# A streaming group-mean subtraction: whole-row tiles, six in-place tiles for four, one sum buffer for two

## The chip, the cores and the metric

The kernel runs on one core of a Trainium2 chip. The metric is the device time in microseconds (us) of that core; profile spans are one to two us shorter than the timed figure of the same kernel. Each kernel was timed in rounds together with the kernel before, on the same chip. A run is marked slow when it is over 1.5% above the fastest of its kernel; the ratios use the other, fast runs alone. The granted clock reads 1.0 in every run here, the slow ones too.

## The reference

```python
x: (8, 4096, 2112) float32, stride 4
pooled    = x.reshape(8, 1024, 4, 2112).mean(axis=2)
upsampled = np.repeat(pooled, 4, axis=1)
return x - upsampled
```

Every group of four neighbouring rows loses its mean. That is 276.8 MB in, 276.8 MB out and very little arithmetic.

## The kernel before

A tile holds 128 groups, one a partition, each group's four rows (33,792 bytes, contiguous in memory) in a line: 64 tiles. SyncE issues the load, VectorE makes three adds and one subtraction in place, ScalarE's queue issues the store. The first and last tile are cut into four quarters by columns.

```python
io_pool  = ctx.enter_context(tc.tile_pool(name="io", bufs=4))
sum_pool = ctx.enter_context(tc.tile_pool(name="sum", bufs=2))
# ... work: whole tiles; the first and the last in EDGE_CHUNKS = 4 column quarters
for g0, gsz, c0, cw in work:
    x_tile = io_pool.tile([P, STRIDE, cw], mybir.dt.float32)
    nc.sync.dma_start(out=x_tile[:gsz], in_=xg[g0:g0 + gsz, :, c0:c0 + cw])
    s = sum_pool.tile([P, cw], mybir.dt.float32)
    nc.vector.tensor_add(out=s[:gsz], in0=x_tile[:gsz, 0, :], in1=x_tile[:gsz, 1, :])
    nc.vector.tensor_add(out=s[:gsz], in0=s[:gsz], in1=x_tile[:gsz, 2, :])
    nc.vector.tensor_add(out=s[:gsz], in0=s[:gsz], in1=x_tile[:gsz, 3, :])
    nc.vector.scalar_tensor_tensor(out=x_tile[:gsz], in0=..., scalar=-1.0 / STRIDE,
                                   in1=x_tile[:gsz], op0=mult, op1=add)   # cut
    nc.scalar.dma_start(out=og[g0:g0 + gsz, :, c0:c0 + cw], in_=x_tile[:gsz])
```

The framework puts in the waits and orders each engine's instructions. With two sum buffers it interleaves two tiles on VectorE.

## Time and profile before

| | before |
|---|---|
| time, median of 3 runs | 1337.71 us (1335.13 to 1340.23) |
| profile span | 1336.5 us |
| DMA over the span | 414 GB/s |
| VectorE busy | 1011.6 us, 76% |

Two views of the kernel before that the prediction doesn't show. The first is the chain that ended last, by engine. The second is the list of DMA issues; its last column is the median time in us from the issue of a transfer to its landing, when all its bytes have arrived.

```profile
DMA 73%; DVE 22%; issue 4%; SPq 0%; DVEq 0%
...
x_tile<-in_x_dram SPq DMA_DIRECT2D x62, 4224.0 KB, 23.1
out_dram<-x_tile ACTq DMA_DIRECT2D x62, 4224.0 KB, 24.1
```

Keep the last two numbers: a load takes 23.1 us and a store 24.1 us, while a tile passes every 20.6 us (990 us of the middle over 48 tiles). So (23.1 + 24.1) / 20.6 = 2.3 whole-tile transfers are outstanding on average, loads and stores together. This number carries the document.

### The profile page before, as it was taken

What the parts mean: (1) busy time and instruction counts of PE and PEld (TensorE: products, weight loads), DVE (VectorE), ACT (ScalarE), POOL (GpSimd) and SP (SyncE); (2) the same over time, 40 slices, a digit from 0 to 9 for tenths busy, and PEclk for the clock granted to TensorE, in tenths of its full rate; (3) what the DMA queues carried; (4) which work ended last, traced back from release to release, by engine and by line L of the source; (5) the groups of instructions that cost most, each with busy time, mean ns of one, the idle gap of its engine ahead of it and who ended that gap; (6) DMA issues with size and microseconds to landing.
All of it is one profiled execution on the core that took longest, in us unless ns stands there. A gap on an engine that the chain in (4) does not pass through costs nothing.

```text
span 1336.5 us, 724 instructions
## 1 busy us (share of the span) xinstructions
DVE 1011.6 (76%) x280; POOL 0.2 (0%) x4
## 2 busy tenths in 40 slices
DVE  5967886787776878695968678776878678796874
POOL 0000000000000000000000000000000000000000
DMA  9999999999999999999999999999999999999987
GB/s 361 383 436 436 430 429 405 417 427 403 436 433 406 417 431 422 433 419 435 405 411 435 420 408 432 392 421 419 408 432 410 434 436 405 436 409 407 433 357 310
DMA packets 26309, 553.70 MB, mean 414 GB/s; under 512 B 2240, under 2 KB 2240, under 8 KB 10432
## 3 DMA queue, kind: packets, MB, share of 16 engines
q1 hardware_dynamic: 13152, 276.83, 50.0%
q10 hardware_dynamic: 13152, 276.83, 48.7%
q14 instruction: 5, 0.04, 0.0%
HBM read 276.82 MB, written 276.82 MB: 414 GB/s over the span
## 4 chain that ended last, share of the span: by engine, by line
DMA 73%; DVE 22%; issue 4%; SPq 0%; DVEq 0%
DMA x_tile<-in_x_dram 40%; DMA out_dram<-x_tile 33%; DVE x_tile L56 16%; DVE s L50 3%; DVE s L53 3%; DVE s L54 1%; SPq L47 0%; DVEq L50 0%; DVEq L56 0%
## 5 line engine op out<-in xcount | busy, mean ns | idle before, releaser
L56 DVE SCALAR_TENSOR_TENSOR x_tile<-s,x_tile 128x8448 f32<-128x8448 f32 (+1 forms) x70 | 573.7, 8196 | 0.3
L50 DVE TENSOR_TENSOR s<-x_tile 128x2112 f32<-128x2112 f32 (+1 forms) x70 | 151.7, 2167 | 318.6 <-DMA x_tile<-in_x_dram 318.6
L53 DVE TENSOR_TENSOR s<-s,x_tile 128x2112 f32<-128x2112 f32 (+1 forms) x70 | 151.4, 2162 | 0.3
L54 DVE TENSOR_TENSOR s<-s,x_tile 128x2112 f32<-128x2112 f32 (+1 forms) x70 | 151.4, 2162 | 0.3
L79 POOL MEMSET const-uint8-127<- 128x1 uint8 x1 | 0.1, 103 | 0.0
L79 POOL MEMSET const-bfloat16-1.0<- 128x1 bf16 x1 | 0.1, 102 | 0.0
L79 POOL MEMSET const-float32-0.0<- 128x1 f32 x1 | 0.1, 99 | 0.2 <-issue 0.2
L79 POOL MEMSET const-float32-1.0<- 128x1 f32 x1 | 0.1, 99 | 0.0
## 6 DMA issues: line engine op xcount, KB each, us to landing
x_tile<-in_x_dram SPq DMA_DIRECT2D x62, 4224.0 KB, 23.1
out_dram<-x_tile ACTq DMA_DIRECT2D x62, 4224.0 KB, 24.1
x_tile<-in_x_dram SPq DMA_DIRECT2D x8, 1056.0 KB, 8.9
out_dram<-x_tile ACTq DMA_DIRECT2D x8, 1056.0 KB, 11.3
```

The source lines that it names most:

```text
L50: nc.vector.tensor_add(out=s[:gsz], in0=x_tile[:gsz, 0, :], in1=x_tile[:gsz, 1, :])
L53: nc.vector.tensor_add(out=s[:gsz], in0=s[:gsz], in1=x_tile[:gsz, 2, :])
L54: nc.vector.tensor_add(out=s[:gsz], in0=s[:gsz], in1=x_tile[:gsz, 3, :])
L56: nc.vector.scalar_tensor_tensor(out=x_tile[:gsz], in0=s[:gsz, None, :].to_broadcast([gsz, STRIDE, cw]), scalar=-1.0 / STRIDE, in1=x_tile[ ...
L79: nc = _bacc.Bacc("TRN2", target_bir_lowering=False, num_devices=1)
```

## The change

The intent of the change: keep more transfers in flight (six tiles), give VectorE one tile at a time so that it holds only one, and drop the small edge transfers. Six tiles and two sum buffers don't fit together: the build then wants 16.5 kB per partition where 9.84 are left. The diff, cut to its core:

```diff
-    io_pool = ctx.enter_context(tc.tile_pool(name="io", bufs=4))
-    sum_pool = ctx.enter_context(tc.tile_pool(name="sum", bufs=2))
+    io_pool = ctx.enter_context(tc.tile_pool(name="io", bufs=IO_BUFS))   # IO_BUFS = 6
+    sum_pool = ctx.enter_context(tc.tile_pool(name="sum", bufs=1))
-    EDGE_CHUNKS = 4
-    ... (work list with quartered first and last tile)
-    for g0, gsz, c0, cw in work:
-        x_tile = io_pool.tile([P, STRIDE, cw], mybir.dt.float32)
-        nc.sync.dma_start(out=x_tile[:gsz], in_=xg[g0:g0 + gsz, :, c0:c0 + cw])
+    for g0 in range(0, G, P):
+        x_tile = io_pool.tile([P, W], mybir.dt.float32)
+        nc.sync.dma_start(out=x_tile[:gsz], in_=xg[g0:g0 + gsz])
     ... (the same three adds and the same subtraction)
```

More of the change, by code (lines that the diff above doesn't have):

```diff
@@ L9 @@
 STRIDE = 4
+IO_BUFS = 6
 @with_exitstack
@@ L23 @@
     G = (B * S) // STRIDE
-    xg = x.rearrange("b (g f) d -> (b g) f d", f=STRIDE)
-    og = out.rearrange("b (g f) d -> (b g) f d", f=STRIDE)
-    n_gtiles = (G + P - 1) // P
-    io_pool = ctx.enter_context(tc.tile_pool(name="io", bufs=4))
-    sum_pool = ctx.enter_context(tc.tile_pool(name="sum", bufs=2))
-    EDGE_CHUNKS = 4
-    work: list[tuple[int, int, int, int]] = []
-    for gt in range(n_gtiles):
-        g0 = gt * P
-        gsz = min(P, G - g0)
-        if gt in (0, n_gtiles - 1):
-            cw = D // EDGE_CHUNKS
-            for ci in range(EDGE_CHUNKS):
-                work.append((g0, gsz, ci * cw, cw))
-        else:
-            work.append((g0, gsz, 0, D))
-    for g0, gsz, c0, cw in work:
-        x_tile = io_pool.tile([P, STRIDE, cw], mybir.dt.float32)
-        nc.sync.dma_start(out=x_tile[:gsz], in_=xg[g0:g0 + gsz, :, c0:c0 + cw])
-        s = sum_pool.tile([P, cw], mybir.dt.float32)
-        nc.vector.tensor_add(
-            out=s[:gsz], in0=x_tile[:gsz, 0, :], in1=x_tile[:gsz, 1, :]
-        )
-        nc.vector.tensor_add(out=s[:gsz], in0=s[:gsz], in1=x_tile[:gsz, 2, :])
-        nc.vector.tensor_add(out=s[:gsz], in0=s[:gsz], in1=x_tile[:gsz, 3, :])
+    W = STRIDE * D
+    xg = x.rearrange("b (g f) d -> (b g) (f d)", f=STRIDE)
+    og = out.rearrange("b (g f) d -> (b g) (f d)", f=STRIDE)
+    io_pool = ctx.enter_context(tc.tile_pool(name="io", bufs=IO_BUFS))
+    sum_pool = ctx.enter_context(tc.tile_pool(name="sum", bufs=1))
+    for g0 in range(0, G, P):
+        gsz = min(P, G - g0)
+        x_tile = io_pool.tile([P, W], mybir.dt.float32)
+        nc.sync.dma_start(out=x_tile[:gsz], in_=xg[g0:g0 + gsz])
+        rows = x_tile[:gsz].rearrange("p (f d) -> p f d", f=STRIDE)
+        s = sum_pool.tile([P, D], mybir.dt.float32)
+        nc.vector.tensor_add(out=s[:gsz], in0=rows[:, 0, :], in1=rows[:, 1, :])
+        for f in range(2, STRIDE):
+            nc.vector.tensor_add(out=s[:gsz], in0=s[:gsz], in1=rows[:, f, :])
         nc.vector.scalar_tensor_tensor(
-            out=x_tile[:gsz],
-            in0=s[:gsz, None, :].to_broadcast([gsz, STRIDE, cw]),
+            out=rows,
+            in0=s[:gsz, None, :].to_broadcast([gsz, STRIDE, D]),
             scalar=-1.0 / STRIDE,
-            in1=x_tile[:gsz],
+            in1=rows,
             op0=mybir.AluOpType.mult,
@@ L63 @@
         )
-        nc.scalar.dma_start(out=og[g0:g0 + gsz, :, c0:c0 + cw], in_=x_tile[:gsz])
+        nc.scalar.dma_start(out=og[g0:g0 + gsz], in_=x_tile[:gsz])
 _INS = ['x']
```

## The prediction

> **What bounds the kernel now.** I read first the busy shares and the DMA rows of the page, then the chain of waits, then the stretches of the span, then the order on VectorE.
>
> ```profile
> span 1336.5 us, 724 instructions
> DVE 1011.6 (76%) x280; POOL 0.2 (0%) x4
> ...
> DMA packets 26309, 553.70 MB, mean 414 GB/s; under 512 B 2240, under 2 KB 2240, under 8 KB 10432
> q1 hardware_dynamic: 13152, 276.83, 50.0%
> q10 hardware_dynamic: 13152, 276.83, 48.7%
> ```
>
> The two queues (q1 loads, q10 stores) are busy 98.7% of the span, VectorE 76%. But 414 GB/s is a mean, so busy is not the same as fast. The stretches show where it is lost; their last two columns are the DMA busy share and GB/s.
>
> ```profile
> 0.00:60.00 60.00, 43.98 (x24) 0.20 (x4) 1.00 0.95 369
> 60.00:240.00 180.00, 134.76 (x35) 0.00 (x0) 1.00 1.00 426
> 240.00:1230.00 990.00, 755.29 (x193) 0.00 (x0) 1.00 1.00 420
> 1230.00:1280.00 50.00, 38.42 (x12) 0.00 (x0) 1.00 1.01 422
> 1280.00:1336.50 56.50, 39.11 (x20) 0.00 (x0) 1.00 0.80 316
> 110.00:150.00 40.00, 40.00 (x12) 0.00 (x0) 1.00 1.00 433
> ```
>
> The last row is an undisturbed stretch: 433 GB/s. At that rate 553.70 MB take 1278.7 us, so 1336.5 - 1278.7 = 57.8 us are lost. By stretch, length x (1 - rate/433): 8.9 at the start, 2.9, 29.7 in the middle, 1.3, and 15.3 at the end. Whether the middle loss can be had back is the whole question, because there the share reads 1.00.
>
> The trace's packet records answer it. A 33,792-byte packet (one partition's row of a tile) takes 1.251 us for the most part; some load packets take up to 2.9 us. They come in bursts: 13 bursts cost 1.0 to 1.5 us each over all 16 engines, some 17 us together, 12 smaller ones about 9 us. Pairing issues with landings, the large bursts stand where both queues had run dry. One of them:
>
> ```profile
> 232.31 8.95 DVE L56 SCALAR_TENSOR_TENSOR x_tile<-s,x_tile 128x8448 f32<-128x8448 f32 x1
> 240.80 0.33 SPq L47 DMA_DIRECT2D x_tile<-in_x_dram  x1
> 241.18 2.35 DVE L54 TENSOR_TENSOR s<-s,x_tile 128x2112 f32<-128x2112 f32 x1
> 241.29 0.34 ACTq L64 DMA_DIRECT2D out_dram<-x_tile  x1
> 243.45 2.35 DVE L50 TENSOR_TENSOR s<-x_tile 128x2112 f32<-128x2112 f32 x1
> ```
>
> At 240.7 a store lands and the only other load in flight has its last packets out; new load and new store are issued within half a microsecond, and that 10 us stretch moves 375 GB/s instead of 433. The cause is buffers: each load waits for a store.
>
> ```profile
> SPq L47 <- DMA out_dram<-x_tile: 1285.2, 66, 25.4
> ```
>
> Counting issues and landings, for about 1010 of the 1336 us only one load is outstanding. Two of the four tiles are often held by VectorE, because with two sum buffers its instructions interleave two tiles:
>
> ```profile
> 165.56 8.95 DVE L56 SCALAR_TENSOR_TENSOR x_tile<-s,x_tile 128x8448 f32<-128x8448 f32 x1
> 174.43 2.35 DVE L53 TENSOR_TENSOR s<-s,x_tile 128x2112 f32<-128x2112 f32 x1
> ...
> 183.44 2.36 DVE L50 TENSOR_TENSOR s<-x_tile 128x2112 f32<-128x2112 f32 x1 [6.65 <-DMA x_tile<-in_x_dram]
> 185.71 2.35 DVE L54 TENSOR_TENSOR s<-s,x_tile 128x2112 f32<-128x2112 f32 x1
> 187.98 2.35 DVE L53 TENSOR_TENSOR s<-s,x_tile 128x2112 f32<-128x2112 f32 x1
> 190.25 8.95 DVE L56 SCALAR_TENSOR_TENSOR x_tile<-s,x_tile 128x8448 f32<-128x8448 f32 x1
> ```
>
> The tile in work at 174.43 needs two adds and the subtraction, 2.4 + 2.4 + 9.0, so could be out at 188.2. It waits in order behind the next tile's first add (183.44), which waits for that tile's load, and ends at 199.2: a buffer held 11 us for nothing.
>
> **What the Trainium skill says.** "DMA: Bandwidth & Descriptors", section "Queues, rings and completion order": each engine alternates between queues that have work, a packet at a time. The trace agrees: from 250 to 260 us both queues moved 2.16 MB. The same page, "Where 436 GB/s comes from", gives a ceiling of 435.2 GB/s; the undisturbed 433 lies just under it, so I treat 433 as the end of the road. "SBUF — State Buffer", "SBUF: two separate sides", holds that DMA and compute engines don't slow each other; at 110 to 150 us VectorE is busy 40.00 of 40.00 and the DMA still makes 433. "Perfetto Trace Analysis", "DMA Optimizations", says splitting transfers may let some start sooner if DMA engines are idle: the argument for the quartered edge tiles, weighed below.
>
> **The change part by part.**
> Quartered edges go. Bytes are the same. Their 8192 packets of 2,112 bytes cost 46.8 us of DMA time (86 ns typical) where whole rows take 2 x 2 x 128 x 1.251 / 16 = 40.0: 6.8 us saved. What is lost is the early first store and short tail.
> Start: four quarter loads fill all four buffers, so the load queue is dry by 14 us and refills late; 8.9 us lost. After, six whole loads are issued at once. First packets at 2.2 us as before; I allow 1.5 for a cold burst. First tile lands near 13.7; VectorE needs 16.1 a tile (the tile begun at 32.93 hands over at 49.10); first store about 30, while 60 us of loads are queued. No gap: loss 3.7 in place of 8.9.
> Middle: two queues with work share 433 GB/s, so a tile passes every 19.98 us (8.65 MB / 433) against 990 / 48 = 20.6 now. VectorE's dependent chain of 16.1 fits, so one tile at a time costs nothing there. Working the first tiles through by hand (store 1 from 32 to 52, store 2 to 72, tile finishes at 46, 62, 78, 94, 110), about two stores, three loads and one tile in VectorE are outstanding from 130 us on, so the load queue never runs dry. The 17 us of large bursts and the idle gaps (29.7 + 2.9 + 1.3 = 33.9, minus 25 in bursts = 9) go; of the 9 us of small bursts, which stand at store handovers, I keep 5.
> End: when the last load lands (T), the store of two tiles earlier has about 9 us left, the next queues behind it to T + 19, and the last tile leaves VectorE at T + 16, its packets ready by T + 18. So the store queue covers the 16 us of VectorE and no gap opens; 1.4 us from last packet to end, as now.
> Sum: 1278.7 + 3.7 + 5 + 1.4 = 1288.8 us of span; runs are timed 1.2 above it (1337.7 against 1336.5): 1290.
>
> **The rivals.**
> 1. DMA already full: 98.7% busy leaves 1.3%, about 1320. For it: the page's share. Against: the share counts slowed packets as busy; GB/s says 4.3% is open. It would hold if the slow bursts came from the memory and not from dry queues; then some 25 us return and the time is 1305 to 1315.
> 2. The edges cost more than I think. If only one store is outstanding at the end, the DMA idles 8 us while VectorE works on the last tile, plus 2 for the issue: 1300. With VectorE two tiles behind, another 16: 1316. Against: at 16.1 per 20.0 it keeps up.
> 3. VectorE becomes the bound: 64 x 16.1 = 1030 plus a first load of 14 and last store of 14, 1058; far off, so it can't set the end.
>
> **Range and chances.** A floor is 1278.7 + 2.2 + 1.4 + 1.2 = 1283.5; little can come out below. Up, residual bursts (up to 25) and tail (10) are not likely both. 1283 to 1308 holds 8 in 10. Faster by over 2% means under 1311: 0.91; within 2%: 0.085; slower: 0.005, as nothing on the bound resource is added.
>
> **What would show it.** Right: the middle at 430 GB/s or more with few packets above 1.3 us; whole-tile loads landing 50 us or more after issue rather than 23 (queued, harmless); VectorE's order one tile at a time with its wait still on loads; some 18,400 packets (64 x 2 x (128 + 16 short ones)) instead of 26,309; start and end each losing under 6 us. Wrong: a middle still near 420 (rival 1), or a last 50 us well below 400 GB/s with the DMA idle during the last subtraction (rival 2).

## The result, and the profile after

The changed kernel takes 1286.62 us, median of 4 runs (1286.50 to 1286.83). The kernel before, over the runs beside it, takes 1336.42 (1327.48 to 1340.23). The ratio is 0.9639, 95% interval 0.9604 to 0.9674. A ratio here is the mean time of one kernel's fast runs over that of the other's of the same rounds, so not quite the ratio of the medians. The new kernel is also steadier: its runs spread over 0.3 us, those of before over almost 13.

Totals and DMA of the changed kernel:

```profile
span 1284.7 us, 674 instructions
DVE 1026.1 (80%) x256; POOL 0.2 (0%) x4
...
DMA packets 18437, 553.70 MB, mean 431 GB/s; under 512 B 2048, under 2 KB 2048, under 8 KB 2048
```

VectorE is busy 14.5 us longer than before and the kernel is 52 us shorter by the spans. The same bytes went at 431 GB/s rather than 414. By stretch (last two columns: DMA busy share and GB/s):

```profile
0.00:60.00 60.00, 46.56 (x12) 0.20 (x4) 1.00 0.98 415
...
240.00:1230.00 990.00, 795.66 (x198) 0.00 (x0) 1.00 1.00 433
1230.00:1280.00 50.00, 32.40 (x9) 0.00 (x0) 1.00 1.00 431
```

The middle row read "1.00 1.00 420" before and reads "1.00 1.00 433" now: the busy share didn't move at all, the rate did. A share of 1.00 is not a full DMA.

The issues and the chain of the changed kernel:

```profile
x_tile<-in_x_dram SPq DMA_DIRECT2D x64, 4224.0 KB, 59.6
out_dram<-x_tile ACTq DMA_DIRECT2D x64, 4224.0 KB, 43.8
```

```profile
DVE 80%; another core or an unknown queue 17%; DMA 1%; issue 1%; DVEq 0%
```

A load now takes 59.6 us, two and a half times as long, and the kernel is faster: the loads wait in line, and the line is what keeps the DMA full. Outstanding are (59.6 + 43.8) / 20.0 = 5.2 transfers. The chain of waits moved from "DMA 73%" to "DVE 80%". Its "unknown queue" is the loads: the list of waits of the changed kernel has VectorE idle for 237.3 us, 18% of the span, all of it for x_tile<-in_x_dram. Whether VectorE has become the bound is asked of an experiment below.

VectorE now does one tile at a time: first add, two adds, subtraction, then the next tile.

```profile
29.23 2.36 DVE L43 TENSOR_TENSOR s<-x_tile 128x2112 f32<-128x2112 f32 x1
31.62 4.75 DVE L45 TENSOR_TENSOR s<-s,x_tile 128x2112 f32<-128x2112 f32 x2
36.40 8.96 DVE L46 SCALAR_TENSOR_TENSOR x_tile<-s,x_tile 128x8448 f32<-128x8448 f32 x1
45.40 2.36 DVE L43 TENSOR_TENSOR s<-x_tile 128x2112 f32<-128x2112 f32 x1
```

### The profile page after: what moved, and what is told of

Its sections match the earlier page's. It is cut to its first block, busy times and chain, and to the rows that moved or that the text cites. A ratio compares the mean times of both kernels' runs of the same rounds, so it can differ in the third digit from the quotient of the medians.

```text
span 1284.7 us, 674 instructions
## 1 busy us (share of the span) xinstructions
DVE 1026.1 (80%) x256; POOL 0.2 (0%) x4
## 2 busy tenths in 40 slices
DMA packets 18437, 553.70 MB, mean 431 GB/s; under 512 B 2048, under 2 KB 2048, under 8 KB 2048
## 4 chain that ended last, share of the span: by engine, by line
DVE 80%; another core or an unknown queue 17%; DMA 1%; issue 1%; DVEq 0%
DVE x_tile L46 45%; DVE s L45 24%; DVE s L43 12%; DMA x_tile<-in_x_dram 1%; DVEq L43 0%
## 5 line engine op out<-in xcount | busy, mean ns | idle before, releaser
L46 DVE SCALAR_TENSOR_TENSOR x_tile<-s,x_tile 128x8448 f32<-128x8448 f32 x64 | 573.3, 8958 | 2.2
L43 DVE TENSOR_TENSOR s<-x_tile 128x2112 f32<-128x2112 f32 x64 | 150.9, 2358 | 237.5 <-DMA x_tile<-in_x_dram 237.3
L45 DVE TENSOR_TENSOR s<-s,x_tile 128x2112 f32<-128x2112 f32 x128 | 301.8, 2358 | 4.4
## 6 DMA issues: line engine op xcount, KB each, us to landing
x_tile<-in_x_dram SPq DMA_DIRECT2D x64, 4224.0 KB, 59.6
out_dram<-x_tile ACTq DMA_DIRECT2D x64, 4224.0 KB, 43.8
```

The lines of the kernel that those rows point to most:

```text
L43: nc.vector.tensor_add(out=s[:gsz], in0=rows[:, 0, :], in1=rows[:, 1, :])
L45: nc.vector.tensor_add(out=s[:gsz], in0=s[:gsz], in1=rows[:, f, :])
L46: nc.vector.scalar_tensor_tensor(out=rows, in0=s[:gsz, None, :].to_broadcast([gsz, STRIDE, D]), scalar=-1.0 / STRIDE, in1=rows, op0=mybir. ...
```

## The experiments

My theory: a tile's buffer goes through load, hold by VectorE (from the landing of the load to the issue of the store), and store. With n buffers and a tile every 20 us, (20 n - hold) / 20 transfers are outstanding. If there are few, both queues run dry from time to time, and the DMA loses time in the dry spell and in the slow packets after it. (The experiments show the first part, that few outstanding transfers cost time; the part on dry spells and slow packets is argued, see the end of the next section.) Measured in the traces, the mean hold between a fifth and nine tenths of the tiles is 34.3 us before and 16.6 us after. The rivals: the number of tiles alone counts; the interleaved order alone counts; the small edge packets are to blame; the slow bursts come from the memory, whatever the queues do; VectorE sets the end.

**One sum buffer, nothing else.**

```diff
-    sum_pool = ctx.enter_context(tc.tile_pool(name="sum", bufs=2))
+    sum_pool = ctx.enter_context(tc.tile_pool(name="sum", bufs=1))
```

> The kernel before with one sum buffer instead of two, nothing else (four tiles, quartered edges). My theory: a tile slot's round is load + hold by VectorE + store, and the DMA runs dry when too few transfers are outstanding; before, four slots x 20.6 us = 82.5 us of round, of which VectorE holds 34.3 us, so 2.33 transfers are outstanding. With one tile at a time the hold falls to about 17 us, so (80 - 17)/20 = 3.15 outstanding: the middle (240 to 1230 us) at 428 GB/s or more, time 1295 to 1305 (the quartered start still loses 9 us). Rival 'only the number of tiles counts': 1330 to 1340, as before. Rival 'VectorE loses by taking tiles one at a time': over 1340.

Measured: 1300.99 us, ratio 0.9764 (0.9713 to 0.9815). The hold fell to 16.3 us. The middle, and the whole-tile issues:

```profile
240.00:1230.00 990.00, 791.80 (x199) 0.00 (x0) 1.00 1.00 433
```

```profile
x_tile<-in_x_dram SPq DMA_DIRECT2D x62, 4224.0 KB, 31.8
out_dram<-x_tile ACTq DMA_DIRECT2D x62, 4224.0 KB, 31.7
```

(31.8 + 31.7) / 20.0 = 3.2 outstanding, and the middle is full with four tiles. So the number of tiles alone doesn't decide.

**Five tiles, nothing else.**

```diff
-    io_pool = ctx.enter_context(tc.tile_pool(name="io", bufs=4))
+    io_pool = ctx.enter_context(tc.tile_pool(name="io", bufs=5))
```

> The kernel before with five tiles instead of four (two sum buffers kept; six do not fit beside them). My theory: a fifth slot pays for the second tile that VectorE holds: (5 x 20 - 34.3)/20 = 3.3 outstanding transfers, so the same as one sum buffer with four tiles: 1293 to 1305, within 5 us of that run, while VectorE still interleaves two tiles. Rival 'the interleaving itself delays the stores and sets the pace': 1325 or more.

Measured: 1296.32 us, ratio 0.9714 (0.9676 to 0.9753).

```profile
240.00:1230.00 990.00, 780.33 (x199) 0.00 (x0) 1.00 1.00 433
```

```profile
x_tile<-in_x_dram SPq DMA_DIRECT2D x62, 4224.0 KB, 28.8
out_dram<-x_tile ACTq DMA_DIRECT2D x62, 4224.0 KB, 35.7
```

VectorE still interleaves two tiles and holds each 33.5 us, as before, but (28.8 + 35.7) / 20.0 = 3.2 are outstanding, and the middle is just as full. So the interleaving doesn't hurt by itself; it costs one buffer. A fifth tile pays that, and one sum buffer saves it. The two parts of the change are two ways to the same 433 GB/s.

**Whole rows at the edges, nothing else.**

```diff
-    EDGE_CHUNKS = 4
+    EDGE_CHUNKS = 1
```

> The kernel before with its edge tiles whole instead of quartered, nothing else. My theory: the middle stays at 420 GB/s with its slow bursts; start and DMA time of the small packets gain some 5 to 10 us, the end may lose as much because one store at most is queued: 1325 to 1342. Rival 'the small packets or the mixed tile sizes set off the dry spells': under 1310.

Measured: 1326.53 us, ratio 0.9942 (0.9917 to 0.9966).

```profile
0.00:60.00 60.00, 46.63 (x12) 0.20 (x4) 1.00 0.99 413
...
240.00:1230.00 990.00, 756.32 (x193) 0.00 (x0) 1.00 1.00 422
```

The start gains 60 x (413 - 369) / 433 = 6.1 us; the middle stays as slow as before (hold 34.4 us, 2.3 outstanding). The small packets didn't cause the dry spells.

**Three tiles, with whole rows and one sum buffer.**

```diff
-IO_BUFS = 6
+IO_BUFS = 3
```

> The changed kernel with three tiles instead of six. My theory: (3 x 20 - 17)/20 = 2.15 outstanding transfers, about as few as before (2.33), so the slow bursts and gaps come back: middle 410 to 422 GB/s, time 1320 to 1345, although VectorE takes one tile at a time and all tiles are whole. Rival 'the single sum buffer and whole rows are what took the loss away, tiles beyond what VectorE needs are idle': under 1300.

Measured: ratio 0.9993 (0.9966 to 1.0020), 20 runs from 1322.47 to 1347.53, the four from 1343.04 up marked slow. The profiled run was one of these, so I ran it again.

> The three-tile run again for a profile in the fast state (before: fast runs at 0.9993 of the kernel before, profile slow at 1342.5). Expected: span 1322 to 1340, middle 415 to 421 GB/s, packet bursts as in the kernel before. Rival 'the bursts of that profile belong to the slow state': middle 430 or more.

Measured: ratio 1.0005 (0.9972 to 1.0038); this profile is a fast run, span 1328.5.

```profile
240.00:1230.00 990.00, 778.23 (x193) 0.00 (x0) 1.00 1.00 423
```

```profile
x_tile<-in_x_dram SPq DMA_DIRECT2D x64, 4224.0 KB, 23.0
out_dram<-x_tile ACTq DMA_DIRECT2D x64, 4224.0 KB, 22.6
```

This is the kernel before in another dress: three tiles with a hold of 16.3 us have as few transfers outstanding, (23.0 + 22.6) / 20.4 = 2.2, as four tiles with a hold of 34.3, and the same time. The middle (423) came out 2 GB/s above what I had written. The time beyond 1.251 us (the usual time of a packet) of all packets, divided by the 16 engines, is 30.9 us in this trace, as in the kernel before. Neither whole rows nor one sum buffer keeps the loss away.

**Four tiles, with whole rows and one sum buffer** (the same line set to 4).

> The changed kernel with four tiles instead of six. My theory: (4 x 20 - 16.3)/20 = 3.2 outstanding transfers, as in the run with one sum buffer only, so the middle is at 433 GB/s; whole rows at the edges take back most of the 10 us by which that run (1301.0) is behind the changed kernel: 1287 to 1294. Rival 'the tiles five and six are needed': 1300 or more.

Measured: 1290.38 us (1290.15 to 1290.46), ratio 0.9662 (0.9641 to 0.9683); middle 433 GB/s. Tiles five and six are worth under 4 us, at the end: with four, the rate of 1230 to 1280 us is 398 GB/s against 431 with six.

**Quartered edges, with six tiles and one sum buffer.**

```diff
-    io_pool = ctx.enter_context(tc.tile_pool(name="io", bufs=4))
-    sum_pool = ctx.enter_context(tc.tile_pool(name="sum", bufs=2))
+    io_pool = ctx.enter_context(tc.tile_pool(name="io", bufs=6))
+    sum_pool = ctx.enter_context(tc.tile_pool(name="sum", bufs=1))
```

> The changed kernel with its edge tiles quartered as before (six tiles, one sum buffer). What the edges alone are worth once the middle is full. My theory: two whole loads now follow the four quarter loads, so the start is no longer dry and loses about 4 to 5 us rather than 9; the slow small packets cost 6.8 us, the end about the same: 1291 to 1298. Rival 'quartered edges shorten the start and the tail': below 1286.

Measured: two fast runs at 1291.19 and 1291.38; two more at 1328.0 and 1376.01, marked slow, the profiled run among them. I don't read that profile. Again:

> The run with quartered edges, six tiles and one sum buffer again, because its profile and one other run fell in a slow state (1328 and 1376 against 1291.2 and 1291.4). Expected: fast runs at 1291.3, 5 us above the changed kernel: start at about 401 GB/s over the first 60 us against 415, that is 2 us, and the small packets' 6.8 us in part. Rival 'quartering and six tiles together are slow by themselves': again over 1300 in most runs.

Measured: four fast runs, 1292.01 to 1298.21, ratio 0.9714 (0.9669 to 0.9758); the profile's middle is at 433 GB/s. With the two fast runs before, that is 4.6 to 11.6 us above the changed kernel, somewhat more than the 5 us I expected. In the profiled run, 10.8 us above, most of it is at the end: after 1230 us it loses 65.5 x (1 - 359/433) = 11.2 us, the changed kernel 4.0. The slow runs didn't return and I have no cause for them.

**Six tiles, stores held back by two tiles, and by three.** The decisive pair: everything of the change is there, only each store is released late. GpSimd adds zero to one column of the old tile, and that zero is made from the tile two (three) further on.

```diff
-        nc.scalar.dma_start(out=og[g0:g0 + gsz], in_=x_tile[:gsz])
+        pending.append((g0, x_tile))
+        while len(pending) > (HOLD if g0 < G - 6 * P else 0):   # HOLD = 2, or 3
+            h0, h_tile = pending.pop(0)
+            if g0 < G - 6 * P:
+                z = z_pool.tile([P, 1], mybir.dt.float32)
+                nc.gpsimd.tensor_scalar_mul(out=z, in0=x_tile[:, 0:1], scalar1=0.0)
+                nc.gpsimd.tensor_add(out=h_tile[:, 0:1], in0=h_tile[:, 0:1], in1=z)
+            nc.scalar.dma_start(out=og[h0:h0 + P], in_=h_tile)
```

> The changed kernel, but each store is released only when VectorE is done with the tile two further on (a touch of one column by GpSimd that adds zero, so the result stays right; the last six tiles are not held). Hold 16.6 + 40 + a few us for the touch, say 57 to 67, so (120 - hold)/20 = 2.7 to 3.1 outstanding. My theory: middle still 430 to 433 GB/s, time 1285 to 1296. Rival 'six tiles and nothing else': the same. Rival 'any delay between VectorE and the store costs': over 1300.

> As the run before it, but held until the tile three further on is done: hold 77 to 87, so 1.7 to 2.1 outstanding transfers, with six tiles, one sum buffer, whole rows and VectorE on one tile at a time. My theory: slow bursts and gaps come back as they were before or worse: middle 405 to 422 GB/s, time 1315 to 1350. Rival 'six tiles are enough whatever holds them' or 'whole rows and one sum keep the bursts away': 1285 to 1296.

Held by two: 1296.82 us, ratio 0.9709 (0.9686 to 0.9733), mean hold 55.9 us. The time is just above the 1285 to 1296 that I had written, the hold just below its 57 to 67; the middle is as expected:

```profile
240.00:1230.00 990.00, 793.12 (x199) 18.26 (x92) 1.00 1.00 433
```

```profile
x_tile<-in_x_dram SPq DMA_DIRECT2D x64, 4224.0 KB, 25.8
out_dram<-x_tile ACTq DMA_DIRECT2D x64, 4224.0 KB, 37.1
```

Held by three: 1348.56 us, ratio 1.0095 (1.0062 to 1.0128), mean hold 77.9 us:

```profile
240.00:1230.00 990.00, 757.43 (x191) 35.88 (x94) 1.00 0.99 416
```

```profile
x_tile<-in_x_dram SPq DMA_DIRECT2D x64, 4224.0 KB, 23.3
out_dram<-x_tile ACTq DMA_DIRECT2D x64, 4224.0 KB, 23.1
```

With 3.1 outstanding the middle is full, with 2.2 it is back at 416, and all the while there are six tiles, whole rows and one sum buffer. GpSimd's touches are in both runs, so they are not the cause. The late first stores cost some time too, which the middle's rates leave out: by two, 60 to 240 us ran at 409 GB/s, and that is most of the 10 us to the changed kernel; by three it ran at 364 GB/s, which is 180 x (1 - 364/433) = 29 us. So compare the middles of this pair, not its total times. A dry spell of the run held by three has the same form as the one in the prediction:

```profile
240.79 0.21 POOL L62 TENSOR_SCALAR z<-x_tile 128x1 f32<-128x1 f32 x1 [24.48 <-DVE x_tile L49]
240.87 0.33 SPq L42 DMA_DIRECT2D x_tile<-in_x_dram  x1
241.08 0.19 POOL L63 TENSOR_TENSOR x_tile<-x_tile,z 128x1 f32<-128x1 f32 x1
241.30 0.34 ACTq L64 DMA_DIRECT2D out_dram<-x_tile  x1
```

A load and a store are issued within half a microsecond, the only other load lands at 242.0, and the stretch from 240 to 250 us makes 335 GB/s.

**VectorE made slower.** One add repeated per tile, then two.

```diff
         nc.vector.tensor_add(out=s[:gsz], in0=rows[:, 0, :], in1=rows[:, 1, :])
+        nc.vector.tensor_add(out=s[:gsz], in0=rows[:, 0, :], in1=rows[:, 1, :])   # once, or twice
```

> The changed kernel with its first add of each tile done twice (2.39 us more of VectorE per tile, same result). The chain of waits of the changed kernel puts 80% of the span on VectorE; if VectorE sets the end, 64 x 2.39 = 153 us more: 1440. My theory: VectorE's 16.17 + 2.39 = 18.56 us per tile still fit in the 19.98 us that the transfers of a tile take: 1286 to 1291.

> As the run before it with two adds more: 16.17 + 4.78 = 20.95 us per tile, now above 19.98. My theory: VectorE becomes the bound: 13 us for the first load, 64 x 20.95 = 1341, 13.6 for the last store, 1.8 to the timed figure: 1365 to 1373. If the room beside the transfers were larger than I think: 1290.

One add more: 1286.64 us, as the changed kernel, with 151 us more of VectorE (1177.0 against 1026.1). Three runs lie at 1286.50 to 1286.70, the profiled one at 1294.47. Its trace shows where it is late: its middle is at 433 GB/s, but from 1270 to 1280 us the DMA moves 68, because the last store is issued at 1279.2, after the packets of the others are almost all out. This is the gap at the end of the prediction's rival 2. Why it opened in this run alone I don't know. Two more: 1368.69 us, ratio 1.0264 (1.0213 to 1.0314), inside the range that the sum 13 + 1341 + 13.6 + 1.8 gave. The run with two adds more:

```profile
DVE 1328.1 (97%) x384; POOL 0.2 (0%) x4
...
240.00:1230.00 990.00, 980.17 (x284) 0.00 (x0) 1.00 1.00 415
```

So the chain's "DVE 80%" was no bound: VectorE had 19.98 - 16.17 = 3.8 us of room in each tile, and the time turned only when that was used up. The last row warns of the opposite error: here VectorE is the bound, and the DMA share still reads 1.00 (at 415 GB/s). It is also the exception to the count of transfers: (41.8 + 34.0) / 21.0 = 3.6 are outstanding, and the rate is low all the same.

Side by side, by the traces' means between a fifth and nine tenths of the tiles (the text above divided medians, which differ by 0.1 at most):

| run | buffers, hold us | outstanding | middle GB/s |
|---|---|---|---|
| held by three | 6, 77.9 | 2.2 | 416 |
| before | 4, 34.3 | 2.3 | 420 |
| whole rows only | 4, 34.4 | 2.3 | 422 |
| three tiles (fast profile) | 3, 16.3 | 2.2 | 423 |
| one sum only | 4, 16.3 | 3.2 | 433 |
| held by two | 6, 55.9 | 3.2 | 433 |
| five tiles only | 5, 33.5 | 3.3 | 433 |
| four tiles, one sum, whole | 4, 16.3 | 3.2 | 433 |
| quartered, again | 6, 16.6 | 5.1 | 433 |
| one add more | 6, 18.7 | 5.1 | 433 |
| changed | 6, 16.6 | 5.2 | 433 |
| two adds more (VectorE the bound) | 6, 50.0 | 3.6 | 415 |

No run stands between 2.3 and 3.2, so where the edge lies between them is open. No variant beat the changed kernel: at 433 GB/s throughout, 553.70 MB take 1278.7 us, and its span of 1284.7 leaves 6 us.

## Why the prediction was right

The predicted time was 1290, measured 1286.62, inside 1283 to 1308.

- **The middle.** Right in its cause, which the held pair shows: few outstanding transfers, not the edges and not VectorE. The size was off by one term: I kept 5 us of the small bursts at store handovers, and the middle lost nothing (433). By the traces' packet records, the time beyond 1.251 us of all packets, divided by the 16 engines, is 30.9 us before and 1.7 us after, and 1.4 us of the latter is two bursts before 35 us. Packets above 1.3 us fell from 917 to 53.
- **The start.** Predicted loss 3.7, measured 60 x (1 - 415/433) = 2.5 us. The first store was to go at about 30 (the prediction's working by hand says 32); it went at 29.2.
- **The end.** The prediction had two stores end 9 and 19 us after the last load lands. In the trace the last load lands at 1254.0 and the last three stores at 1264.0, 1274.0 and 1283.9. No gap opened. The rates charge 4.0 us to the stretch after 1230 (0.2 to 1280, 3.8 after it) where I had allowed 1.4 for the wait after the last packet; that wait was 1.1. For the rest, the last packets don't end together: most by 1281.5, the last at 1283.6.
- **The sum.** 1278.7 + 2.5 + 0 + 4.0 = 1285.2, which is the span of 1284.7 within rounding. The prediction had 1288.8: 5 too much in the middle and 1.2 at the start, 2.6 too little at the end. The timed figure lies 1.8 us above the span where 1.2 was added. So the errors offset in part, and 1290 is nearer to the measured time than its terms are.
- **Rival 1** (DMA already full; slow bursts from the memory) is out: the bursts went when the queues were kept full, and came back with the stores held by three tiles.
- **Rival 2** (dearer edges) is out for the changed kernel: whole edges gained, 0.9942 by themselves, and no gap opened at its end. The gap exists, though: the late run with one add more has it.
- **Rival 3** (VectorE) is out, as I had said: at 16.2 us per tile it isn't the bound, nor at 18.6; at 21.0 it is.
- **What I had not seen:** that the parts overlap almost wholly. I credited six tiles and the single sum together with the middle; a fifth tile alone, or the single sum alone, fills it. Six tiles over four are worth 4 us once the single sum is there.

One thing stays open: how few outstanding transfers cost the time. By the packet records, slow packets are most of it: of the 29.7 us that the middle lost before, 24.7 are time beyond 1.251 us, and 741 of the 917 packets above 1.3 us are loads. Why they are slow no run shows. Dry queues can't be the whole reason: with two adds more, at least one load and one store are outstanding at every moment of the middle, and the time beyond 1.251 us is 38.6 us there. VectorE leaves the DMA time to spare in that run, so its trace can't tell whether the slow packets cost time or only fill it.

## What to carry to other kernels

In a streaming kernel, add the median issue-to-landing times of loads and stores and divide by the time per tile: the number of transfers outstanding. Near two, this DMA ran at 416 to 423 GB/s with a busy share of 0.99 to 1.00; above three, at 433, as long as VectorE was not the bound (with it, 3.6 and 415). Before buying buffers, look at how long the compute engine holds each one: the interleaving held each tile 18 us longer (34.3 against 16.3), nearly the 20 us of one buffer, and a fifth buffer made up for it.

## What the Trainium skill lacked or had wrong

- No page says how many transfers must be outstanding to keep the DMA full. Here 2.2 to 2.3 of 4.3 MB give 416 to 423 GB/s; 3.2 and more give 433 where VectorE is not the bound.
- "Trainium Kernel Development and Optimization", section "Best Practices", says to double-buffer so that DMA and compute overlap. That falls short for an in-place load, compute and store: three tiles gave 0.9993 of the time of the kernel before, four with a short hold 0.9662. No run here has two.
- "DMA: Bandwidth & Descriptors", section "Where 436 GB/s comes from", says that for transfers between HBM (the chip's main memory) and SBUF (the core's own memory, where the tiles lie) the HBM side, about 358 GB/s, binds. Read alone, this sentence misleads: the one core of this program sustained 433 GB/s over 990 us, reads and writes counted together. The same section also calls 425 GB/s, measured with 16 MB, near the fabric's rate, and that fits.
